# One-hot operations of the experts against a row of numbers in PSUM, four tokens at a time for the first kind, and GELU's result left in PSUM

## Chip, cores, metric

The kernel runs on one core of a Trainium2 chip. A core has TensorE (PE in the profile, its weight loads PEld), VectorE (DVE), ScalarE (ACT), GpSimd (POOL) and a queue for transfers (SP). The metric is device time in microseconds of one execution of the whole kernel.

## What is computed

A transformer of three layers on 256 tokens of width 1024, in float32. Two layers form the first block; the third, the second block, ends in the experts that this case is about. Each token takes 8 heads with 16 of 16384 rows of two tables each, picked by a product of two sets of 128 keys:

```python
def body(hblk):
    q = (hblk @ w_q).reshape(B, TB, PEER_HEADS, 2, PEER_DHALF)
    s = jnp.einsum('btphd,phnd->btphn', q, subkeys).astype(jnp.float32)
    v, i = lax.top_k(s, PEER_TOPK)
    ...
    tv, tj = lax.top_k(cand, PEER_TOPK)
    eidx = jnp.take_along_axis(cidx, tj, axis=-1)
    w = jax.nn.softmax(tv, axis=-1)
    u = w_down[eidx]
    a = jax.nn.gelu(jnp.einsum('btd,btpkd->btpk', hblk, u).astype(jnp.float32))
    vv = w_up[eidx]
    return jnp.einsum('btpk,btpkd->btd', (w * a).astype(hblk.dtype), vv)
```

So a token has 128 pairs (row, column) in a grid of 128 by 128 experts, and a weight for each.

## The kernel before

**Dense experts.** The kernel gathers nothing. It treats the grid as 128 units of 128 experts. For unit `e`, `expert(e)` multiplies the unit's part of `w_down` with h for all 256 tokens: 24 matmuls of 128x256 (three for each of 8 slices of the width, lines 284 to 286, since each operand is split in two float32r parts). `gelu(e, o)` applies GELU to the result o, which lies in one of the PSUM banks 0 to 3 in turn. The result, times the token's weight for each expert, stands in `slots[e]` (128 experts x 256 tokens). After all 128 units, `finish` multiplies the slots with `w_up`.

**Weights of a token.** In the later part of the 128 units, the kernel also builds each token's 128x128 grid of weights: the product of two one-hot matrices. `onehot(t)` makes both on VectorE, each from one `tensor_scalar` over `con`, a tile that holds 0 to 127 in each row: line 1639 compares it with the token's 128 row numbers (one per partition, in `SELT[:, 0, t]`), line 1640 compares it with the column numbers and multiplies by the weights. `weight(t)` is one float32 matmul of the two (line 1648, two records in the trace), into a quarter of one of the banks 4 to 7. When four tokens (a group) fill a bank, `place` distributes it: for the units that have their GELU, VectorE multiplies (line 1657); for the later ones ScalarE copies (line 1659). For a later unit, `gelu` then has two parts: tokens without weights as before (line 1566), tokens with weights through a buffer `gls` in SBUF (line 1569), which VectorE multiplies into the slot (line 1570).

**Order.** Every engine works through its instructions in the order of the program. `expert` calls `token` four times, after each second slice (six matmuls); `token` issues `onehot(t + 3)` and then `weight(t)` when one is due, at a rate that spreads 256 tokens over the units that are left. Here the first weight stands with 81.6 units to go, so 0.79 tokens fall on a call. The stretch from the first weight matmul to the last is called the token stage below.

**Loads.** Each unit's 512 KB come by a transfer into one of four buffers, ScalarE writes the upper part (line 238), and GpSimd the rest (line 240: source minus upper part, both in SBUF). In the stage of `finish` VectorE does that subtraction (line 242).

Of the kernel before, what the change touches and what calls it, by code (L numbers as in the profile page):

```python
# [16 lines left out]
P = 128  # L17
# [13 lines left out]

# ---------------------------------------------------------------- constants of the shapes
def shape_constants():
# [64 lines left out]

# ---------------------------------------------------------------- layout of the inputs
def lay_out(i):  # L100
# [72 lines left out]

# ---------------------------------------------------------------- the stream of weights
RG_YIELD = (1,)
# [3 lines left out]
class Stream:  # L179
    """Weights in the order of their use: loaded ahead, split ahead into two float32r parts."""  # L180

# [18 lines left out]
    def free(self, which, u):  # L200
        """Whether all that reads unit u from its buffer is in the program."""
        return u < 0 or (u < self.done if which == 1 and self.units[u][3] else u < self.busy)

    def buf(self, i, which):
        """The buffer of the ring whose last user is the longest gone, if it is free."""
        r = [x for x in self.rings if x[0] <= i][-1][which]
        j = min(range(len(r)), key=lambda j: self.last.get((which, r[j][0]), -1))
        key = (which, r[j][0])
        if not self.free(which, self.last.get(key, -1)):
            return None  # L210
        self.last[key] = i
        return r[j][1]
# [33 lines left out]
    def take(self, labels):  # L246
        """Units that are used together."""
        self.busy = self.pos
        us = [self.next(*l, hold=True) for l in labels]
        return us  # L250
# [22 lines left out]
class Build:  # L273
    def __init__(self, ctx, tc, I, out, dbg):
        self.ctx, self.tc, self.nc, self.I, self.out, self.dbg = ctx, tc, tc.nc, I, out, dbg

    # ------------------------------------------------------------ helpers
    def dump(self, name, ap):
# [33 lines left out]

    # ------------------------------------------------------------ the whole program
    def run(self):
# [93 lines left out]

    # ------------------------------------------------------------ modulations
    def mods_setup(self, mp):  # L410
# [16 lines left out]
    def first_mods(self):  # L427
        """The first two modulations, on the tensor engine: the rows of silu(c) in two parts, the weights moving."""
        nc, I, W = self.nc, self.I, self.W
# [55 lines left out]
    def dot(self, l, jt, w):  # L485
        """One tile of a modulation: its rows times the row of silu(c)."""
        nc = self.nc
        junk = self.mp.tile([P, D], BF16, name=f"junk{l}_{jt}", tag="junk", bufs=1)
        if l == 2:
            outs = [(2, self.mad2[:, jt:jt + 1])]  # L490
        else:
            outs = [(c, self.mall[:, l, c, jt:jt + 1]) for c in ((0, 1) if l == 0 or jt < 40 else (0,))]
        for c, o in outs:
            nc.vector.scalar_tensor_tensor(junk, w, 1.0, self.cb[c], op0=OP.mult, op1=OP.mult, accum_out=o)  # L494
# [7 lines left out]
    def more(self, pool, end, n=2, stagger=False):  # L502
        """Two more buffers for split weights in a pool that is open until the unit `end`."""
        W = self.W
        self.nmore = getattr(self, "nmore", 0) + 1
        new = [(f"m{self.nmore}_{j}", pool.tile([P, 2, 1024], F32R, name=f"hm{self.nmore}_{j}", bufs=1)) for j in range(n)]
        e = W.index(*end)
        W.ring(W.done, self.raws, self.hls + new)
        if stagger:
            W.ring(e - 4, self.raws, self.hls)  # L510
            W.ring(e - 2, self.raws, new)
        W.ring(e, self.raws, self.hls)
# [59 lines left out]

    # ------------------------------------------------------------ norm and modulation of x into h
    def norm(self, T, l, i):
        """Prepares h = rms(x) * s1 + s0 for the next linear map; l, i name the modulation."""
        self.nT, self.nl, self.ni = T, l, i
        self.ndouble = l == 2 and i == 0
        self.nacc = self.np.tile([P, 512], F32, name="nacc", tag="nacc", bufs=1)
        self.nlast = self.np.tile([P, 512], F32, name="nlast", tag="nlast", bufs=1)
        self.nrow = {}  # L580
        self.nsq, self.nadd = [self.nlast], self.nc.gpsimd
# [38 lines left out]
    def bcast(self, half):  # L620
        """One over the root mean square of each token, in all partitions."""
        R, cols = self.nrow[half]
        rows = [R[:, :P], R[:, P:]] + ([self.bank[7][:, S + j * P:S + (j + 1) * P] for j in range(2)] if self.ndouble else [])
        for o, c in zip(rows, cols):
            self.nc.tensor.matmul(o, c.broadcast_to((P, P)), self.C["ident"], start=True, stop=True)
# [30 lines left out]

    # ------------------------------------------------------------ linear maps
    def group(self, labels, T, early=False):
        """First tiles of a linear map of h, with k outside: it starts with the first rows of h.
        The columns of x run while those of the context are normalised."""  # L660
        W = self.W
# [36 lines left out]
    def tail(self, label, nk, T, gate, last=True, order=None, rest=None):  # L698
        """x += gate * (w^T g): d tiles; the last ones by halves, so that the next norm overlaps them."""
        nc = self.nc  # L700
# [72 lines left out]

    # ------------------------------------------------------------ feed forward
    def ffn(self, l, w, T, nxt, fp, early=False):
# [26 lines left out]

    # ------------------------------------------------------------ first block
    def first_block(self):
# [314 lines left out]

    # ------------------------------------------------------------ second block: retention and sparse attention  # L1120
    def second_mix(self):
        nc, tc, I, W = self.nc, self.tc, self.I, self.W
        T = S
        with tc.tile_pool(name="mix2", bufs=1) as p:
# [55 lines left out]
            def tokens(u, k, c0, n, o):  # L1180
                """Rows of h as the stationary side: n columns from c0 of the unit, for both tiles of tokens."""
                for t in range(2):
# [16 lines left out]
            def blocks(kv):  # L1199
                """The raw keys or values of the blocks, two rows of a block on top of each other."""  # L1200
                Y = p.tile([P, 2, T], F32, name=f"Y{kv}")
# [327 lines left out]

    # ------------------------------------------------------------ second block: the experts  # L1530
    def peer(self, fb):
# [8 lines left out]
        SELT = Xf[:, 0, :768].rearrange("p (a t) -> p a t", a=3)  # L1540
        gls = [Xf[:, 0, 1280:1536], Xf[:, 0, 1536:1792]]
        con = pp.tile([P, P], F32, name="iota")
# [19 lines left out]
        def gelu(e, o):  # L1562
# [4 lines left out]
            if nb:  # L1567
                g = gls[e % 2]
                nc.scalar.activation(g[:, :nb], o[:, :nb], AF.Gelu_apprx_tanh)
            return lambda: nb and nc.vector.tensor_tensor(slots[e][:, :nb], slots[e][:, :nb], g[:, :nb], OP.mult)  # L1570

# [55 lines left out]
        self.ring = [0, 1, 2, 3]  # L1627
        wb = [4, 5, 6, 7]
        SAv = self.SA.rearrange("p (e t) -> p e t", t=S)
        SCv = Xf[:, 0:1, 1792:2048]  # L1630
        SBv = slotB.rearrange("p (e t) -> p e t", t=S)

        ohs = {}

        def onehot(t):
            if t >= T:
                return
            oh = pp.tile([P, 2, P], F32, name="oh", tag="oh", bufs=4)
            nc.vector.tensor_scalar(oh[:, 0], con, SELT[:, 0, t:t + 1], None, op0=OP.is_equal)  # L1639
            nc.vector.tensor_scalar(oh[:, 1], con, SELT[:, 1, t:t + 1], SELT[:, 2, t:t + 1], op0=OP.is_equal, op1=OP.mult)  # L1640
            ohs[t] = oh

        def weight(t):
            if t >= T:
                return
            oh = ohs.pop(t)
            o = self.bank[wb[t // 4 % 4]][:, t % 4 * P:(t % 4 + 1) * P]
            nc.tensor.matmul(o, oh[:, 0], oh[:, 1], start=True, stop=True)  # L1648

        def place(g, e):  # L1650
            """The weights of four tokens go to all experts: those up to e have their activations."""
            bv = self.bank[wb[g % 4]].rearrange("p (t e) -> p e t", e=P)
            ts = slice(4 * g, 4 * g + 4)
# [49 lines left out]
    def topk(self, p, iota, SC, SEL):  # L1703
        """The experts of all tokens and their weights; yields about the vector engine's time in us."""
        nc = self.nc
# [66 lines left out]
    def finish(self, slots, xd, pp):  # L1772
# [17 lines left out]
        def ends():  # L1790
            """What the end needs, in the place of slots that have been used."""
            nc.sync.dma_start(SA[:, :2048], xd)
# [51 lines left out]

# ---------------------------------------------------------------- launch
# [13 lines left out]
```

## Time and profile before

| | before |
|---|---|
| timed runs, median of 3 | 2833.49 us (2833.3 to 2834.64) |
| span of the profiled execution | 2830.7 us |
| TensorE busy | 2731.6 us (97%) |
| VectorE busy | 1903.9 us (67%) |
| GpSimd busy | 505.6 us (18%) |
| bytes read from HBM | 446.35 MB, 158 GB/s over the span |

The span goes from the first to the last instruction. For the profiled execution the profile gives the span and no other time; the median of the timed runs lies 2.8 us above that span. A matmul's record is longer than the distance to the next one, since matmuls are pipelined: "busy" counts the union of the records.

### The profile page before, as it was taken

How to read it: one execution, taken by the hardware profiler on the slowest of the kernel's cores; microseconds unless marked ns; L12 is line 12 of the kernel's file. 1: busy time of each engine (PE TensorE's matmuls, PEld its weight loads, DVE VectorE, ACT ScalarE, POOL GpSimd, SP SyncE). 2: the span in 40 equal slices, each digit the busy share in tenths (PEclk: the TensorE clock that was granted, in tenths of full speed). 3: DMA queues.
4: the chain of work that ended last, by engine and by line, in shares of the span. 5: the costliest groups of instructions: out<-in, count | busy, mean ns of one | idle time of the engine just before them, and what ended most of it. 6: DMA issues, size and time to landing. Idle time of an engine off the chain costs nothing. (4 is left out here: it accounts for less than half of the span.)

```text
span 2830.7 us, 41128 instructions
## 1 busy us (share of the span) xinstructions
PE 2731.6 (97%) x15899; PEld 2352.1 (83%) x15899; DVE 1903.9 (67%) x3580; ACT 1089.4 (38%) x1867; POOL 505.6 (18%) x284
## 2 busy tenths in 40 slices
PE   6999999999999999999999999999999988899998
PEld 4888887678888898888978999779998988888887
DVE  6777764457776565555546556675888999855555
ACT  5322234433222232222344444634443443354554
POOL 1000010020000010000121002331896555400000
PEclk9999999999999999999999999999999999999999
DMA  6555643124555535555344555424554434456664
GB/s 252 183 191 187 194 126 110 54 82 142 184 185 192 175 126 189 191 193 182 110 127 129 191 185 171 161 68 164 181 163 142 133 122 134 129 193 207 193 193 142
DMA packets 129477, 451.41 MB, mean 159 GB/s; under 512 B 16000, under 2 KB 21120, under 8 KB 127744
## 3 DMA queue, kind: packets, MB, share of 16 engines
q1 hardware_dynamic: 129280, 448.77, 49.2%
q8 instruction: 125, 2.05, 0.3%
q14 instruction: 72, 0.59, 0.1%
HBM read 446.35 MB, written 2.10 MB: 158 GB/s over the span
## 5 line engine op out<-in xcount | busy, mean ns | idle before, releaser
L284 PE MATMUL bank<-Hh,hl 128*128 128x256 f32 (+1 forms) x1968 | 663.2, 337 | 6.9 <-ACT Hh L643 5.1
L286 PE MATMUL bank<-Hh,hl 128*128 128x256 f32 (+1 forms) x1968 | 641.9, 326 | 2.7 <-POOL hl L240 2.7
L285 PE MATMUL bank<-Hl,hl 128*128 128x256 f32 (+1 forms) x1968 | 642.6, 327 | 1.7 <-DVE Hl L646 1.6
L238 ACT ACTIVATE hl<-raw 128x1024 fp32r<-128x1024 f32 (+1 forms) x401 | 411.7, 1043 | 280.3 <-DMA raw<-in_w_dram 84.7
L242 DVE TENSOR_TENSOR hl<-raw,hl 128x1024 fp32r<-128x1024 f32 (+1 forms) x316 | 381.4, 1216 | 184.6 <-ACT hl L238 183.9
L284 PEld LDWEIGHTS bank<-Hh,hl 128*128 128x128 f32 x1968 | 375.3, 191 | 51.2 <-issue 11.2
L286 PEld LDWEIGHTS bank<-Hh,hl 128*128 128x128 f32 x1968 | 375.0, 191 | 36.2 <-POOL hl L240 3.3
L285 PEld LDWEIGHTS bank<-Hl,hl 128*128 128x128 f32 x1968 | 375.4, 191 | 34.2 <-DVE Hl L646 2.7
L494 DVE SCALAR_TENSOR_TENSOR junk<-wm,cb 128x1024 bf16<-128x1024 f32 x272 | 332.0, 1221 | 12.2 <-ACT cb L500 7.7
L597 POOL TENSOR_TENSOR nacc<-nlast,nacc 128x256 f32<-128x256 f32 (+1 forms) x56 | 60.9, 1093 | 1342.6 <-issue 848.8
L240 POOL TENSOR_TENSOR hl<-raw,hl 128x1024 fp32r<-128x1024 f32 x85 | 214.6, 2532 | 194.6 <-ACT hl L238 181.9
L284 PE MATMUL bank<-G,hl 128*128 128x512 f32 (+1 forms) x673 | 229.6, 341 | 0.0
L285 PE MATMUL bank<-G,hl 128*128 128x512 f32 (+1 forms) x673 | 228.6, 340 | 0.0
L286 PE MATMUL bank<-G,hl 128*128 128x512 f32 (+1 forms) x673 | 228.5, 340 | 0.0
L310 ACT ACTIVATE G<-silu 128x512 fp32r<-128x512 f32 (+1 forms) x88 | 50.9, 579 | 414.1 <-DVE silu L783 414.1
L783 DVE TENSOR_TENSOR silu<-silu,bank 128x512 f32<-128x512 f32 (+1 forms) x88 | 54.6, 621 | 201.9 <-PE bank L286 197.1
L1807 PE MATMUL bank<-hl,Hh 128*128 128x512 f32 x768 | 179.4, 389 | 0.0
L284 PE MATMUL bank<-Hh,hm 128*128 128x512 f32 (+1 forms) x496 | 177.4, 358 | 0.0
L286 PE MATMUL bank<-Hh,hm 128*128 128x512 f32 (+1 forms) x496 | 177.1, 357 | 0.0
L285 PE MATMUL bank<-Hl,hm 128*128 128x512 f32 (+1 forms) x496 | 176.9, 357 | 0.0
L709 DVE SCALAR_TENSOR_TENSOR X<-bank,mall,X 128x256 f32<-128x256 f32 x192 | 84.5, 479 | 132.8 <-PE bank L286 132.7
L1807 PEld LDWEIGHTS bank<-hl,Hh 128*128 128x128 f32 x768 | 144.2, 188 | 29.9
(350 smaller groups left out, 5327.0 us busy)
## 6 DMA issues: line engine op xcount, KB each, us to landing
raw<-in_w_dram SPq DMA_DIRECT2D x208, 512.0 KB, 4.1
wm<-in_wmod_dram SPq DMA_DIRECT2D x128, 512.0 KB, 4.3
X<-in_wdn_dram SPq DMA_DIRECT2D x64, 512.0 KB, 3.6
raw<-in_wdn_dram SPq DMA_DIRECT2D x64, 512.0 KB, 3.6
X<-in_wup_dram SPq DMA_DIRECT2D x64, 512.0 KB, 3.6
raw<-in_wup_dram SPq DMA_DIRECT2D x64, 512.0 KB, 3.7
raw<-in_w_dram SPq DMA_DIRECT2D x64, 448.0 KB, 3.8
wm<-in_wada_dram SPq DMA_DIRECT2D x48, 512.0 KB, 4.6
```

What stands on the lines that cost most here:

```text
L238: nc.scalar.activation(hl[:, 0, :n], raw[:, :n], AF.Copy)
L240: nc.gpsimd.tensor_tensor(hl[:, 1, :n], raw[:, :n], hl[:, 0, :n].bitcast(F32), OP.subtract)
L242: nc.vector.tensor_tensor(hl[:, 1, :n], raw[:, :n], hl[:, 0, :n].bitcast(F32), OP.subtract)
L284: mm(o, wh, xh, start=start, stop=False)
L285: mm(o, wh, xl, start=False, stop=False)
L286: mm(o, wl, xh, start=False, stop=stop)
L310: nc.scalar.activation(dst[0], src, AF.Copy)
L494: nc.vector.scalar_tensor_tensor(junk, w, 1.0, self.cb[c], op0=OP.mult, op1=OP.mult, accum_out=o)
L597: self.nadd.tensor_tensor(acc, last, acc, OP.add)
L709: nc.vector.scalar_tensor_tensor(x, self.bank_(b, T, half), g[:, d:d + 1], x, op0=OP.mult, op1=OP.add)
L783: nc.vector.tensor_tensor(s, s, self.bank_(bb, T), OP.mult)
L1807: nc.tensor.matmul(acc[t][n], c[:, a, ts], u[:, b, n * 512:(n + 1) * 512], start=e == 0 and a + b == 0, stop=e == P - 1 and a == 1)
```

## The change

`io` is a copy of `con` in bank 4 of PSUM. Both kinds of one-hot matrix are compared with `io`. The first kind is made for four tokens by one `tensor_tensor` of 512 columns, into one of two buffers in X; the second kind stays one `tensor_scalar` per token, now into one of six buffers of its own (four of the double size before). The weights of a group go to three banks in turn, 5 to 7. GELU's result for the tokens with weights overwrites o in its bank, and the multiplication reads it there; `gls` goes.

```diff
-        gls = [Xf[:, 0, 1280:1536], Xf[:, 0, 1536:1792]]
...
-                g = gls[e % 2]
+                g = o
                 nc.scalar.activation(g[:, :nb], o[:, :nb], AF.Gelu_apprx_tanh)
-            return lambda: nb and nc.vector.tensor_tensor(slots[e][:, :nb], slots[e][:, :nb], g[:, :nb], OP.mult)
+            return lambda: nb and nc.vector.tensor_tensor(slots[e][:, :nb], g[:, :nb], slots[e][:, :nb], OP.mult)
...
-        wb = [4, 5, 6, 7]
+        io = self.bank[4][:, :P]
+        nc.vector.tensor_copy(io, con)
+        wb = [5, 6, 7]
...
-            oh = pp.tile([P, 2, P], F32, name="oh", tag="oh", bufs=4)
-            nc.vector.tensor_scalar(oh[:, 0], con, SELT[:, 0, t:t + 1], None, op0=OP.is_equal)
-            nc.vector.tensor_scalar(oh[:, 1], con, SELT[:, 1, t:t + 1], SELT[:, 2, t:t + 1], op0=OP.is_equal, op1=OP.mult)
+            if t % 4 == 0:
+                first = Xf[:, 0, 768 + t // 4 % 2 * 512:][:, :512].rearrange("p (t e) -> p t e", t=4)
+                nc.vector.tensor_tensor(first, io.unsqueeze(1).broadcast_to((P, 4, P)),
+                                        SELT[:, 0, t:t + 4].unsqueeze(2).broadcast_to((P, 4, P)), OP.is_equal)
+                firsts[t // 4] = first
+            oh = pp.tile([P, P], F32, name="oh", tag="oh", bufs=6)
+            nc.vector.tensor_scalar(oh, io, SELT[:, 1, t:t + 1], SELT[:, 2, t:t + 1], op0=OP.is_equal, op1=OP.mult)
...
-            o = self.bank[wb[t // 4 % 4]][:, t % 4 * P:(t % 4 + 1) * P]
-            nc.tensor.matmul(o, oh[:, 0], oh[:, 1], start=True, stop=True)
+            o = self.bank[wb[t // 4 % 3]][:, t % 4 * P:(t % 4 + 1) * P]
+            nc.tensor.matmul(o, firsts[t // 4][:, t % 4], oh, start=True, stop=True)
...
-            bv = self.bank[wb[g % 4]].rearrange("p (t e) -> p e t", e=P)
+            bv = self.bank[wb[g % 3]].rearrange("p (t e) -> p e t", e=P)
```

On VectorE, between the places where units 56 and 57 have their weights, there stood before (line, operation, what it writes and reads, size; in brackets the engines waited for):

```order
L1570 TENSOR_TENSOR slotA_14610<-slotA_14610,X_71 128x28 [waits Activation_49]
L1657 TENSOR_TENSOR slotA_14610<-slotA_14610,bank7_70 128x56x4
L1639 TENSOR_SCALAR oh_17158<-iota_14606,X_71 128x128 [waits PE_49]
L1640 TENSOR_SCALAR oh_17158<-iota_14606,X_71 128x128
L1639 TENSOR_SCALAR oh_17168<-iota_14606,X_71 128x128 [waits PE_49]
L1640 TENSOR_SCALAR oh_17168<-iota_14606,X_71 128x128
L1639 TENSOR_SCALAR oh_17184<-iota_14606,X_71 128x128 [waits PE_49]
L1640 TENSOR_SCALAR oh_17184<-iota_14606,X_71 128x128
L1570 TENSOR_TENSOR slotA_14610<-slotA_14610,X_71 128x32 [waits Activation_49]
L1657 TENSOR_TENSOR slotA_14610<-slotA_14610,bank4_67 128x57x4
```

and now, at the same place (lines 1569, 1642, 1646 and 1663 of the changed kernel are the GELU product, the four tokens' first one-hot matrices, the second kind and the product of `place`):

```order
L1569 TENSOR_TENSOR slotA_14610<-bank2_65,slotA_14610 128x28 [waits Activation_49]
L1663 TENSOR_TENSOR slotA_14610<-slotA_14610,bank6_69 128x56x4
L1642 TENSOR_TENSOR X_71<-bank4_67,X_71 128x512 [waits PE_49]
L1646 TENSOR_SCALAR oh_17130<-bank4_67,X_71 128x128 [waits DVE_49]
L1646 TENSOR_SCALAR oh_17139<-bank4_67,X_71 128x128 [waits DVE_49]
L1646 TENSOR_SCALAR oh_17154<-bank4_67,X_71 128x128 [waits PE_49]
L1569 TENSOR_TENSOR slotA_14610<-bank3_66,slotA_14610 128x32 [waits Activation_49]
L1663 TENSOR_TENSOR slotA_14610<-slotA_14610,bank7_70 128x57x4
L1646 TENSOR_SCALAR oh_17173<-bank4_67,X_71 128x128 [waits PE_49]
```

Three tokens' six operations on `iota` (`con`) have become one on four tokens and four single ones, all of which read bank 4. The GELU product reads a bank where it read X. A one-hot operation waited for the matmul of four tokens back to give its buffer free; now the operation on four tokens waits for the last weight matmul of two groups back, and a single one for that of six tokens back.

On TensorE, where a group's first weight stands, before:

```order
L285 MATMUL bank3_66<-Hl_73,Hh_72 128x256
L286 MATMUL bank3_66<-Hh_72 128x256
L1648 MATMUL bank4_67<-oh_17266 128x128 [waits DVE_49,Activation_49]
L284 MATMUL bank3_66<-Hh_72 128x256
L285 MATMUL bank3_66<-Hl_73,Hh_72 128x256
```

and now:

```order
L285 MATMUL bank3_66<-Hl_73,Hh_72 128x256
L286 MATMUL bank3_66<-Hh_72 128x256
L1654 MATMUL bank5_68<-oh_17232,X_71 128x128 [waits DVE_49,Activation_49]
L284 MATMUL bank3_66<-Hh_72 128x256
L285 MATMUL bank3_66<-Hl_73,Hh_72 128x256
```

Nothing has moved on TensorE. The matmul reads two tiles where it read one, and the ScalarE copy that it waits for is that of the group three back, before four back.

## Rows read from the trace of the kernel before

**Rows 1.** The page's first part, whole span: busy us, share, count.

```profile
PE 2731.6 (97%) x15899; PEld 2352.1 (83%) x15899; DVE 1903.9 (67%) x3580; ACT 1089.4 (38%) x1867; POOL 505.6 (18%) x284
```

**Rows 2.** Chain that ended last, through the token stage: share by line.

```profile
by line: DVE oh L1639 31.5%; DVE oh L1640 30.9%; PE bank L1648 6.6%; PE bank L284 6.5%; PE bank L285 6.3%; PE bank L286 6.3%; DVE slotA L1657 4.2%; DVE slotB L1570 4.2%; DVE slotB L1657 2.0%; issue 1.1%; DVE Hl L242 0.4%; ACT Hl L238 0.3%; 
```

**Rows 3.** Busy time by window: the token stage, a slice of it, and one before.

```profile
core 0: us, PE busy (x) PEld busy (x) DVE busy (x) ACT busy (x) POOL busy (x), PEclk, DMA share, GB/s
2131.43:2465.79 334.36, 300.74 (x2470) 293.09 (x2471) 320.61 (x699) 129.07 (x381) 188.38 (x79) 0.99 0.42 129
2140.00:2160.00 20.00, 19.70 (x168) 19.50 (x168) 18.61 (x40) 8.52 (x27) 12.00 (x6) 1.00 0.41 129
2040.00:2060.00 20.00, 20.00 (x169) 20.00 (x168) 20.00 (x89) 9.31 (x14) 19.24 (x9) 1.00 0.77 218
```

**Rows 4.** That slice for line 1648 alone: PE busy, PEld busy, clock, DMA.

```profile
2140.00:2160.00 20.00, 6.62 (x34) 5.22 (x34) 1.00 0.41 129
```

**Rows 5.** Waits in the token stage: total us, times, longest.

```profile
ACT slotB L1659 <- DVE slotB L1657: 141.4, 45, 6.7
PE bank L1648 <- DVE oh L1640: 33.6, 38, 1.7
```

**Rows 6.** Lines 1639 and 1640: duration ns min/median/max, first and last start.

```profile
L1639 DVE TENSOR_SCALAR oh<-iota,X x256: 268/276/2459, 2128.6 to 2464.7; 128x128 f32<-128x128 f32 x128
L1640 DVE TENSOR_SCALAR oh<-iota,X x256: 329/335/2541, 2128.9 to 2464.9; 128x128 f32<-128x128 f32 x128
```

**Rows 7.** VectorE by line, token stage: count, busy us, mean ns, idle before.

```profile
L1640 DVE TENSOR_SCALAR oh<-iota,X 128x128 f32<-128x128 f32 x255 | 159.0, 623 | 0.0
L1639 DVE TENSOR_SCALAR oh<-iota,X 128x128 f32<-128x128 f32 x255 | 148.0, 580 | 10.6 <-PE bank L1648 10.2
L1657 DVE TENSOR_TENSOR slotA<-slotA,bank 128x272 f32<-128x272 f32 (+16 forms) x63 | 26.1, 414 | 0.0
L1570 DVE TENSOR_TENSOR slotB<-slotB,X 128x80 f32<-128x80 f32 (+45 forms) x58 | 22.4, 386 | 0.0
L1657 DVE TENSOR_TENSOR slotB<-slotB,bank 128x4 f32<-128x4 f32 (+44 forms) x45 | 11.8, 263 | 0.0
```

**Rows 8.** Timeline around 2267: GpSimd, VectorE, TensorE (start, us, engine, line).

```profile
2265.33 2.41 POOL L240 TENSOR_TENSOR Hl<-X,Hl 128x1024 fp32r<-128x1024 f32 x1 [3.40 <-ACT Hl L238]
2267.69 2.36 POOL L240 TENSOR_TENSOR hl<-raw,hl 128x1024 fp32r<-128x1024 f32 x1
...
2265.44 2.38 DVE L1639 TENSOR_SCALAR oh<-iota,X 128x128 f32<-128x128 f32 x1
2267.74 2.40 DVE L1640 TENSOR_SCALAR oh<-iota,X 128x128 f32<-128x128 f32 x1
...
2268.38 0.28 PE L286 MATMUL bank<-Hh 128*128 128x256 f32 x1
2270.20 0.49 PE L1648 MATMUL bank<-oh 128*128 128x128 f32 x2 [1.54 <-DVE oh L1640]
```

**Rows 9.** Timeline around 1899: GpSimd, then VectorE, in an earlier stage.

```profile
1898.69 2.50 POOL L240 TENSOR_TENSOR hl<-raw,hl 128x1024 fp32r<-128x1024 f32 x1
...
1898.89 0.72 DVE L1508 TENSOR_SCALAR ry<-bank,mv,rr 128x128 f32<-128x128 f32 x2
1899.65 1.83 DVE L1510 TENSOR_TENSOR ry<-ry,RG 128x256 f32<-128x256 f32 x1
```

**Rows 10.** Line 1508 (ns min/median/max), and line 783 by shape.

```profile
L1508 DVE TENSOR_SCALAR ry<-bank,mv,rr x8: 401/404/410, 1871.7 to 1906.7; 128x128 f32<-128x128 f32 x8
...
L783 DVE TENSOR_TENSOR silu<-silu,bank 128x512 f32<-128x512 f32 x66 | 45.4, 688 | 169.6 <-PE bank L286 166.5 <-ACT silu L782 3.1
```

**Rows 11.** ScalarE by line, token stage.

```profile
L238 ACT ACTIVATE hl<-raw 128x1024 fp32r<-128x1024 f32 x40 | 43.2, 1080 | 0.0
L1569 ACT ACTIVATE X<-bank 128x4 f32<-128x4 f32 (+39 forms) x79 | 23.4, 296 | 0.0
L1659 ACT ACTIVATE slotB<-bank 128x236 f32<-128x236 f32 (+45 forms) x62 | 18.4, 296 | 145.8 <-DVE slotB L1657 141.4 <-DVE slotA L1657 4.4
```

More of the change, by code (lines that the diff above doesn't have):

```diff
@@ L1631, in peer @@
         SBv = slotB.rearrange("p (e t) -> p e t", t=S)
-        ohs = {}
+        ohs, firsts = {}, {}
         def onehot(t):
```

## The prediction, made before the changed kernel ran

> **What bounds the kernel now.** The page comes first: TensorE is busy 97% of the span, VectorE 67% [rows 1]. Read alone, that says that VectorE's work costs nothing. It is an average over stages, so the next view is the chain of waits through the token stage. There the chain runs 31.5% through line 1639 and 30.9% through line 1640, the two one-hot operations, and only about 6.5% through each line of matmuls [rows 2]. In this stage TensorE follows VectorE.
>
> The windows give the stage its size: 334.36 us, 2470 matmul records, TensorE busy 300.74, VectorE 320.61 (96%), GpSimd 188.38 in 79 operations [rows 3]. TensorE is idle 33.6 us, and the waits give all of it to one cause: the weight matmul waits for a one-hot matrix 38 times [rows 5].
>
> Why is VectorE so busy? A one-hot operation takes 276 ns (line 1639) or 335 (line 1640) at the median, but up to 2459 and 2541 [rows 6], and 580 and 623 in the mean [rows 7]. The timeline shows what the long ones have in common: GpSimd starts its subtraction at 2265.33 and works to 2267.74; a one-hot operation that starts at 2265.44 ends at 2267.82. GpSimd's next runs from 2267.69 to 2270.05, and line 1640's goes from 2267.74 to 2270.14. The weight matmul behind them starts at 2270.20, 1.82 us after the matmul ahead of it [rows 8]. A one-hot operation that meets GpSimd's subtraction stands still until that ends. The bill for the stage: lines 1639 and 1640 take 148.0 + 159.0 = 307.0 us [rows 7], and would take 255 x (0.276 + 0.335) = 155.8 at their medians. The 151 us between are 1.9 us for each of GpSimd's 79 operations: nearly every one holds VectorE for most of its 2.4 us.
>
> **The change, step by step.**
>
> 1. *Does a source in PSUM escape?* Line 1508 is the operation that the second kind becomes: `tensor_scalar`, 128x128, source in a bank, two columns of scalars in SBUF, result in SBUF. Two of them start at 1898.89, inside a GpSimd subtraction (1898.69 to 1901.19), and both are done in 0.72 us; line 1510 behind them, with two sources in SBUF, takes 1.83 us and ends with GpSimd [rows 9]. All eight took 401 to 410 ns [rows 10]. The four-token operation has one source in a bank and one in SBUF, as line 1657 has, whose mean is 414 ns for up to 272 columns, with no long ones in the mean [rows 7]. The GELU product takes that form too. So I take the stall as gone for all three.
>
> 2. *VectorE's own work.* The second kind goes from 335 to 404 ns [rows 6, 10]. The first kind for four tokens is priced by line 783, a product of 512 columns with one source in a bank: 688 ns [rows 10]; bounds are 0.6 (1.5 times line 1657's) and 1.1 us (four times line 1639's median). Four tokens cost 4 x (276 + 335) = 2444 ns before without stalls, and 688 + 4 x 404 = 2304 now. So the merging as such saves 0.14 us a group, 9 us in 64 groups of an engine that is then no longer waited for: nothing. The stage's sum on VectorE becomes 64 x 0.688 + 256 x 0.404 + 26.1 + 11.8 (`place`) + 22.4 (GELU product, as now) = 208 us.
>
> [...]
>
> 3. *TensorE at its own pace.* The slice from 2140 to 2160 has almost no wait: 168 records with 19.70 us busy [rows 3], 34 of them weight matmuls [rows 4]. That is 20.2%, against 512 of 2470 = 20.7% for the stage, so its mix is right. At 168 per 20.00 us the stage takes 2470 / 8.40 = 294.0 us; at 168 per 19.70 it takes 289.6. I take the middle, 292, and a gain of 334.4 - 292 = 42.4. It is more than the 33.6 us of idle, because a matmul's record goes on for some time into each wait.
>
> 4. *What is late next?* The feeding must hold a unit (24 + 6.3 records) every 3.6 us where it held one every 4.1. GpSimd needs 188 of 292 us. ScalarE needs 129 [rows 3]; now it mostly waits for VectorE's product (141.4 us, [rows 5]), and its splits stand behind that, so it is freed too. The slice from 2040 to 2060, before the stage, shows units without weight matmuls: 169 records in 20.00 us with TensorE never idle, at 218 GB/s and with GpSimd busy 19.24 [rows 3]. Feeding at 129 x 334 / 292 = 148 GB/s is well inside that. VectorE at 208 of 292 is the fullest of the three.
>
> 5. *New waits.* A group's first weight now waits for ScalarE's copies of the group three back, not four. Those copies stand, at the latest, behind the GELU of unit e-1 when the earlier group ended in unit e; the weight stands at least six matmuls into e for that group's last token, and five tokens later, at 0.79 tokens for six matmuls: at least 36 more. So there are 42 matmuls, 42 x 20 / 168 = 5.0 us, and the weights between them, 6 x 2 x 20 / 168 = 1.4. In that time ScalarE must do the GELU's two parts (0.26 for the part in the slot, taken as 0.3; 0.296), a split (1.08), and up to three copies (0.3 each), and VectorE the GELU product (0.39) and `place` (0.41 + 0.26) [rows 7, 11]: 3.6 us together. It fits with 2.8 us over. The bank of a GELU result is free only after VectorE's product; its next user is four units later. The buffers of the one-hot matrices got longer, six and eight tokens against four. GELU's write to a bank instead of SBUF has no row; even 0.1 us either way, 79 times, is 8 us of ScalarE's idle 205.
>
> 6. *Start.* One copy into bank 4 and the first operation on four tokens stand ahead of the first weight: at most 0.41 (a `place` product of twice its columns) + 0.69 + 0.40, less the 0.61 of before, 0.9 us once. I count 0.5.
>
> Sum: -42.4 + 0.5, about -42. In the profile's terms 2830.7 becomes 2788.7; the timed median lies 2.8 us above the span, so 2833.5 - 42 = **2791.5 us**.
>
> **Rivals.**
>
> *TensorE stays half starved* (chance 0.11). One in-order VectorE serves TensorE, ScalarE and the slots; a product that waits for a GELU holds back the one-hot matrices queued behind it. VectorE stands only three tokens ahead in the program, 3 x 292 / 256 = 3.4 us. For it: VectorE now waits 10.2 us in all before line 1639 for the matmul that frees a buffer [rows 7], so it is ahead at times and late at others. Against it: without stalls it is 71% busy. If half the gain is lost: 2833.5 - 21 = 2812.
>
> *The change doesn't do what it says* (0.04). Scalars and one input still come from SBUF. If GpSimd holds such operations too, the bill of 1.9 us for each subtraction stays, VectorE's own work is the same within 9 us, and the time is 2833 within 5. Against it stand the two operations in rows 9, few as they are.
>
> *Slower: three banks* (0.03). If ScalarE's copies came later than the 6.4 us of step 5, TensorE would wait at each group's first weight, 61 times. ScalarE's longest wait for VectorE is 6.7 us now [rows 5], but that one is made by the stalls that go. To be slower by over 0.2% it must eat the gain and 5.7 us more, 48 us, so 0.8 us at every group, copies at 7.2 us or later. At 1 us a group the time would be 2833.5 - 42 + 61 = 2852.
>
> **How the numbers follow.** The forecast, that TensorE runs the stage at its own pace, has the rest, 0.82. Its own range comes from step 3: at 289.6 us and no start cost 2788.7; at 294.0 us and 0.9 us, 2794. If only the idle time of 33.6 us comes back, 2800. Since a tenth of the chance lies near 2812 and some of the forecast's may lie just above its own range, I give 2785 to 2802. A change of 0.2%, 5.7 us, is about what a measurement of this kernel can tell from none. Faster by more than that: 0.82 + 0.11 = 0.93; within it 0.04; slower 0.03.
>
> **What the profile after should show.** The two kinds of one-hot operation with a mean within 5% of their median, about 404 and 690 ns, and no 2.4 us among them, though GpSimd's subtractions still take 2.4. VectorE busy near 208 us in the token stage, which lasts 290 to 296 us. The waits of the weight matmul for a one-hot matrix below 5 us. ScalarE's wait for VectorE's product smaller, its wait for the end of a unit on TensorE larger. The chain of waits through the stage on the matmul lines. The prediction is wrong if one-hot operations still reach 2.4 us (step 1), if VectorE's chain is still there without stalls (step 2), or if weight matmuls wait for ScalarE (step 5); outside the token stage nothing should move by more than a microsecond or two.

## The result, and the profile after

The changed kernel takes 2789.68 us (median of 4 runs, 2787.89 to 2790.71) against 2833.39 before (median of 4, 2829.94 to 2834.64): a ratio of 0.984, 95% interval 0.983 to 0.986. The forecast was 2791.5.

The page's first part of the changed kernel (busy us, share of the span, count):

```profile
span 2786.0 us, 40945 instructions
...
PE 2721.2 (98%) x15899; PEld 2348.9 (84%) x15899; DVE 1760.2 (63%) x3389; ACT 1103.4 (40%) x1867; POOL 506.5 (18%) x284
```

TensorE's busy time has fallen by 10 us and its share risen by a point; VectorE has lost 144 us. The page alone would not say which of these bought 44.7 us of span. The chain of waits through the token stage does:

```profile
by line: PE bank L284 26.3%; PE bank L285 26.2%; PE bank L286 26.1%; PE bank L1654 19.4%; DVE oh L1646 0.4%; DVE Hl L242 0.4%; ACT Hl L238 0.4%; DVE slotA L1663 0.2%; DVE slotB L1569 0.2%; issue 0.1%; DVE slotB L1663 0.1%; ACT slotB L1665 0
```

In [rows 2] the two one-hot lines had 62% of the stage's chain; now line 1646 has 0.4%, and the four lines of TensorE have 98%. The window of the token stage (from the first weight matmul to the last; busy us and count by engine, granted clock, DMA share, GB/s):

```profile
core 0: us, PE busy (x) PEld busy (x) DVE busy (x) ACT busy (x) POOL busy (x), PEclk, DMA share, GB/s
2128.25:2421.16 292.91, 291.52 (x2470) 291.32 (x2471) 177.81 (x507) 142.56 (x381) 190.22 (x80) 1.00 0.48 148
```

Against [rows 3]: the same 2470 matmul records in 292.91 us where they took 334.36. TensorE is idle 1.4 us of it, where it was idle 33.6. VectorE is busy 178 us where it was busy 321. GpSimd's time has not changed.

The two kinds of one-hot operation, by line (duration in ns: minimum, median, maximum):

```profile
L1646 DVE TENSOR_SCALAR oh<-bank,X x256: 394/402/414, 2127.7 to 2420.2; 128x128 f32<-128x128 f32 x128
```

```profile
L1642 DVE TENSOR_TENSOR X<-bank,X x64: 681/691/692, 2127.1 to 2414.7; 128x512 f32<-128x512 f32 x64
```

This answers to [rows 6]: the maximum is 414 ns where it was 2541, though GpSimd's 80 subtractions fill 65% of the stage. The waits in the stage (total us, times, longest):

```profile
DVE X L1642 <- PE bank L1654: 90.4, 61, 2.2
ACT slotB L1565 <- PE bank L286: 70.7, 50, 2.2
ACT slotB L1665 <- DVE slotB L1663: 33.4, 26, 3.8
DVE oh L1646 <- PE bank L1654: 16.1, 36, 1.0
PEld bank L1654 <- DVE oh L1646: 1.6, 1, 1.6
```

Who waits for whom has turned round. VectorE now waits for TensorE, 90 us before the four-token operation and 16 before the single one, for its buffers. TensorE's weight matmul waits once for VectorE, 1.4 us (its weight load, the last row, 1.6); in [rows 5] it waited 33.6. The slots lie in two tiles, slotA and slotB: for those in slotB, ScalarE's wait for VectorE's product in `place` went from 141 to 33 us, and its line 1565 waits 71 us for the end of a unit on TensorE.

### The profile page after: what moved, and what is told of

It reads as the page before. It is cut to its first block, busy times and chain, and to the rows that moved or that the text cites. A ratio compares the mean times of both kernels' runs of the same rounds, so it can differ in the third digit from the quotient of the medians.

```text
span 2786.0 us, 40945 instructions
## 1 busy us (share of the span) xinstructions
PE 2721.2 (98%) x15899; PEld 2348.9 (84%) x15899; DVE 1760.2 (63%) x3389; ACT 1103.4 (40%) x1867; POOL 506.5 (18%) x284
```

## Experiments

The prediction's account: operations of VectorE with all their tensors in SBUF stand still while GpSimd subtracts; with one source in PSUM they don't; the four-token operation, the longer buffers, the three banks and the GELU part have next to no share. The rivals: the merging or the buffers did it; VectorE's queue remains a bound; three banks cost something. Times are medians; the kernel before beside the first four runs took 2833.4 (13 runs), beside the last four 2838.4 (9 runs, 2828.6 to 2843.6).

**The row of numbers back in SBUF.** Edit of the changed kernel:

```diff
-        io = self.bank[4][:, :P]
-        nc.vector.tensor_copy(io, con)
+        io = con
```

> The changed kernel, with the row of numbers read from its tile in SBUF again; one operation for four tokens, the longer buffers, three banks and GELU's result in PSUM stay. If operations with all sources in SBUF are held by GpSimd's subtraction (the prediction's account), the long one-hot operations of 2.4 us come back, VectorE is above 95% busy in the token stage, that stage takes 325 to 340 us and the kernel 2818 to 2838. If the gain came from fewer operations or longer buffers, it stays at 2790 within 4.

Measured: 2826.5 us, ratio to before 0.997 (0.995 to 0.998). The window of its token stage, with the columns of the window above, the two one-hot lines by busy us and mean ns, and the wait of the weight matmul:

```profile
2134.54:2460.40 325.86, 303.84 (x2470) 299.99 (x2471) 307.23 (x507) 138.48 (x381) 195.64 (x79) 0.97 0.42 132
```

```profile
L1645 DVE TENSOR_SCALAR oh<-iota,X 128x128 f32<-128x128 f32 x255 | 197.6, 815 | 1.1 <-PE bank L1653 1.1
L1641 DVE TENSOR_TENSOR X<-iota,X 128x512 f32<-128x512 f32 x63 | 74.7, 1186 | 9.9 <-PE bank L1653 9.8
```

```profile
PE bank L1653 <- DVE oh L1645: 17.5, 12, 3.3
```

The stage is back at 326 us with VectorE 94% busy (above 95% was expected). The means are 815 and 1186 ns; 255 x 0.334 + 63 x 0.680 = 128 us at their own medians (334 and 680), so of 272 us, 144 are standing still: 1.8 us for each of GpSimd's 79 operations, against 1.9 before. Fewer operations did not lower that bill. What the merging, the longer buffers, the three banks and GELU's result in PSUM give together without the PSUM source is 7 us; which of them, this run doesn't tell.

The 7 us are not the worth of the shorter waiting alone. TensorE is idle 22.0 us of the stage where it was idle 33.6, but the granted clock of the stage is 0.97 where it was 0.99 before. The waits for a one-hot matrix have become fewer and longer: 12 of up to 3.3 us, where [rows 5] has 38 of up to 1.7. What a granted clock below 1 is for the matmuls, the profile of the kernel before shows once: after the 1.97 us that TensorE waited ahead of its first weight, matmuls of 256 columns stand 0.21 us apart from 2132.2 to 2135.4, where they are else 0.12 apart, and the profile gives 0.50 for the clock of that stretch, 0.83 for the 10 us from 2130. That is 1.7 us of missing clock; every later 10 us of that stage has 1.00. By its 0.97 the run here misses 0.03 x 325.86 = 10 us, an estimate from a rounded figure (8 to 11). After which of its waits the clock falls was not shown.

**The row of numbers in PSUM, and nothing else.** Edit of the kernel before:

```diff
-        wb = [4, 5, 6, 7]
+        io = self.bank[4][:, :P]
+        nc.vector.tensor_copy(io, con)
+        wb = [5, 6, 7]
...
-            nc.vector.tensor_scalar(oh[:, 0], con, SELT[:, 0, t:t + 1], None, op0=OP.is_equal)
+            nc.vector.tensor_scalar(oh[:, 0], io, SELT[:, 0, t:t + 1], None, op0=OP.is_equal)
...
-            nc.vector.tensor_scalar(oh[:, 1], con, SELT[:, 1, t:t + 1], SELT[:, 2, t:t + 1], op0=OP.is_equal, op1=OP.mult)
+            nc.vector.tensor_scalar(oh[:, 1], io, SELT[:, 1, t:t + 1], SELT[:, 2, t:t + 1], op0=OP.is_equal, op1=OP.mult)
```

(and the remainder by 3 in place of 4 in `weight` and `place`, since bank 4 is taken).

> The kernel before, with the row of numbers in bank 4 and three banks for the weights, and nothing else: two operations per token, four buffers, GELU's result through SBUF. If the held operations are the cause, this alone gives nearly all of the gain: 2788 to 2797, one-hot operations at about 345 and 404 ns with no long ones, while some of the 80 GELU products, still with two sources in SBUF, now take up to 2.5 us. If the merging is what counts, the time stays within 6 us of 2833.

Measured: 2792.4 us, ratio 0.985 (0.982 to 0.988). Window of its token stage, and lines of VectorE:

```profile
2132.58:2425.83 293.25, 290.46 (x2469) 289.71 (x2470) 264.20 (x700) 129.56 (x381) 193.16 (x80) 1.00 0.48 148
```

```profile
L1642 DVE TENSOR_SCALAR oh<-bank,X 128x128 f32<-128x128 f32 x255 | 101.5, 398 | 0.0
L1641 DVE TENSOR_SCALAR oh<-bank,X 128x128 f32<-128x128 f32 x255 | 87.1, 341 | 25.9 <-PE bank L1650 25.2
L1570 DVE TENSOR_TENSOR slotB<-slotB,X 128x80 f32<-128x80 f32 (+45 forms) x58 | 59.2, 1021 | 0.0
L1570 DVE TENSOR_TENSOR slotA<-slotA,X 128x8 f32<-128x8 f32 (+15 forms) x21 | 24.2, 1153 | 0.0
```

This one step gives 41 of the 44 us. Line 1642 (the second kind) and line 1641 (the first) have means of 398 and 341 ns. GpSimd's hold has moved to what is left with two sources in SBUF: the GELU products have means of 1021 and 1153 ns, 83.4 us in all where they took 26.2 (22.4 in [rows 7] and 3.8 in slotA). VectorE is 90% busy, and TensorE still hardly waits (it is idle 2.8 us of the stage).

**GELU's result through SBUF again.** Edit of the changed kernel (with two tiles `gls` of 256 columns, and `bufs=4` for the second kind):

```diff
-                g = o
+                g = gls[e % 2]
...
-            return lambda: nb and nc.vector.tensor_tensor(slots[e][:, :nb], g[:, :nb], slots[e][:, :nb], OP.mult)
+            return lambda: nb and nc.vector.tensor_tensor(slots[e][:, :nb], slots[e][:, :nb], g[:, :nb], OP.mult)
```

> The changed kernel, with GELU's result through two buffers in SBUF as before (and four buffers of the second one-hot kind instead of six, for the room). By the prediction's account the products are held by GpSimd now, up to 2.5 us each, perhaps 40 of 80, some 50 us of VectorE's time; but VectorE has 115 us to spare in the token stage, so the time stays at 2788 to 2795. If the products' place on VectorE's in-order queue matters, the weight matmul waits again and the time is above 2800.

Measured: 2791.4 us, ratio 0.985 (0.982 to 0.988). Window of its token stage:

```profile
2129.06:2424.00 294.94, 291.76 (x2470) 291.39 (x2471) 243.07 (x507) 129.63 (x381) 190.56 (x80) 1.00 0.48 147
```

VectorE's busy time rises by 65 us, the stage by 2, the kernel by 1 to 2 us, which the runs hardly tell from nothing. So the GELU part of the change is work off the path.

**GpSimd's subtraction on a quarter of the columns.** Edit of the kernel before:

```diff
-                    nc.gpsimd.tensor_tensor(hl[:, 1, :n], raw[:, :n], hl[:, 0, :n].bitcast(F32), OP.subtract)
+                    m = n // 4 if label[0] == "wdn" else n
+                    nc.gpsimd.tensor_tensor(hl[:, 1, :m], raw[:, :m], hl[:, 0, :m].bitcast(F32), OP.subtract)
```

> The kernel before, in which GpSimd subtracts only 256 of the 1024 columns of each unit of the down weights; the other columns keep what the buffer held, so the experts' products are not the reference's. VectorE's instructions are those of before. If GpSimd's subtraction is what holds the one-hot operations, they are held 0.6 us at most, VectorE falls to about 220 to 240 us in the token stage, and the kernel takes 2788 to 2800. If the long operations have another cause, it stays at 2833 within 6.

Measured: 2781.1 us, ratio 0.981 (0.979 to 0.984). Window of its token stage, and the one-hot lines:

```profile
2124.10:2414.97 290.87, 289.37 (x2470) 289.17 (x2471) 194.14 (x699) 130.74 (x381) 59.98 (x79) 1.00 0.47 148
```

```profile
L1641 DVE TENSOR_SCALAR oh<-iota,X 128x128 f32<-128x128 f32 x255 | 91.5, 359 | 0.0
L1640 DVE TENSOR_SCALAR oh<-iota,X 128x128 f32<-128x128 f32 x255 | 80.5, 316 | 93.5 <-PE bank L1649 92.7
```

VectorE's program is that of the kernel before, with everything in SBUF; only GpSimd holds it for less long. The stage falls to 290.9 us, and the one-hot means to 316 and 359 ns. So it is GpSimd's operation that holds VectorE, and a shorter one holds it less: over the medians of the kernel before, the one-hot lines now stand 16 us (80.5 + 91.5 - 155.8), 0.2 us for each subtraction of 0.76 us, where it was 1.9 us for one of 2.4. The bill fell by more than the length did; VectorE is idle for 93 us of this stage and so less often in the way, which is an argument and was not measured. The expected time was missed by 7 us on the low side and VectorE's 220 us by 26: the shorter subtractions also help ahead of the token stage (the first weight stands at 2124.1 us, in the two profiles of the changed kernel at 2128.2 and 2131.0). There no matmul of the units waits for GpSimd's subtraction in this run; in the kernel before those of line 286 wait 5.2 us for it, and TensorE is busy 24.79 of the 30.00 us between 2080 and 2110. The last run below takes up that stretch.

**Four banks for the weights.** The changed kernel, run again as the measure for the next three runs:

> The changed kernel itself, as the measure for the three runs beside it: 2789 within 3.

Measured: 2790.5 us (5 runs, 2787.8 to 2791.4). The edit:

```diff
-        self.ring = [0, 1, 2, 3]
+        self.ring = [0, 1, 2]
...
-        wb = [5, 6, 7]
+        wb = [3, 5, 6, 7]
```

(and the remainder by 4 in place of 3 in `weight` and `place`; the units' products have three banks for it.)

> The changed kernel with four banks for the weights and three instead of four for the units' products. If three banks cost nothing (the prediction's step 5), the time is that of the changed kernel within 3 us. If weight matmuls lose time on ScalarE's copies, it is lower by more than 3.

Measured: 2790.5 us. Window of its token stage:

```profile
2130.51:2423.45 292.94, 291.54 (x2470) 291.35 (x2471) 177.97 (x507) 142.57 (x381) 190.19 (x80) 1.00 0.48 148
```

Nothing moves, neither the stage nor the waits in it: three banks were enough.

**The second kind twice.** The changed kernel, in which line 1646 stands twice in a row:

> The changed kernel, in which each one-hot operation of the second kind is done twice, into the same buffer: 256 operations more of 0.40 us, about 0.32 apart. VectorE goes from 178 to about 260 us busy of the stage's 293. If VectorE is off the path (the prediction), the time stays within 4 us of the changed kernel; if TensorE follows VectorE's queue even without stalls, it rises by 20 us or more.

Measured: 2791.9 us, 1.4 more than the changed kernel. Window of its token stage, and the wait of the weight matmul:

```profile
2129.16:2424.78 295.62, 291.76 (x2470) 291.39 (x2471) 272.92 (x762) 141.62 (x381) 190.10 (x80) 1.00 0.48 147
```

```profile
PE bank L1655 <- DVE oh L1647: 3.9, 2, 3.1
```

VectorE has 95 us more to do, is busy 273 us of 295.6 (about 260 were expected), and the stage is 2.7 us longer; a single wait of 3.1 us ahead of the last weights is about that much. With no stalls in it (means of 403 and 410 ns for the two lines), a VectorE that is 92% busy still feeds TensorE; before, one that was 96% busy with stalls of 2.4 us in it cost 33.6 us of idle.

**The same step just ahead of the token stage.** In the changed kernel's profile TensorE was idle 5.2 us between 2080 and 2110, where VectorE chooses the experts. The window (busy us by engine, clock, DMA), GpSimd's timeline and VectorE's, of the changed kernel:

```profile
2080.00:2110.00 30.00, 24.79 (x198) 23.77 (x198) 29.83 (x13) 14.10 (x21) 30.00 (x9) 1.00 0.43 130
```

```profile
2076.92 4.57 POOL L240 TENSOR_TENSOR Hh<-X,Hh 128x1024 fp32r<-128x1024 f32 x1
2081.44 4.43 POOL L240 TENSOR_TENSOR Hl<-X,Hl 128x1024 fp32r<-128x1024 f32 x1
```

```profile
2076.94 2.28 DVE L1760 TENSOR_TENSOR cand<-abf,iota 128x2048 f32<-128x2048 f32 x1
2079.25 4.38 DVE L1763 TENSOR_TENSOR cand<-cand,i16f 128x2048 f32<-128x2048 f32 x1
```

Here each holds the other. The comparison of line 1760, two sources in SBUF, is through in 2.28 us, and GpSimd's subtraction beside it takes 4.57, to 2081.49. The product of line 1763 stands until then and takes 4.38, to 2083.63, and GpSimd's next one stands until that and takes 4.43. The edit, in `topk` of the changed kernel, puts the indices and the 16 numbers in banks 6 and 7, which are free by then:

```diff
-        v16, i16, i16f = two("v16", [P, 16, 16]), two("i16", [P, 16, 16], U32), two("i16f", [P, 16, 16])
+        v16, i16 = two("v16", [P, 16, 16]), two("i16", [P, 16, 16], U32)
+        i16f = [self.bank[6][:, t * S:(t + 1) * S].rearrange("p (a n) -> p a n", a=16) for t in range(2)]
+        nc.vector.tensor_copy(self.bank[7][:, :16], iota[:, :16])
...
-        io = iota[:, :16].unsqueeze(1).broadcast_to((P, P, 16))
+        io = self.bank[7][:, :16].unsqueeze(1).broadcast_to((P, P, 16))
```

> The changed kernel, with the same step taken in the choice of the experts, just ahead of the token stage: the 16 numbers and the indices that its four comparisons and four products of 2048 columns read go to two banks. In the changed kernel's profile GpSimd's subtractions take up to 4.5 us there and TensorE is idle 5.2 us between 2080 and 2110. If those are held by VectorE's two sources in SBUF, GpSimd's stay at 2.4, the comparisons and products fall from 3.9 and 4.4 to 2.3 us, and the kernel gains 4 to 6 us: 2784 within 3. If GpSimd is late there for another reason, it stays at 2789.

Measured: 2783.9 us (5 runs, 2780.0 to 2785.3), 6.6 below the changed kernel's 2790.5 beside it, with no overlap of the runs. The window of 2080 to 2110, GpSimd's timeline and the two lines of VectorE:

```profile
2080.00:2110.00 30.00, 30.00 (x253) 30.00 (x252) 21.72 (x14) 17.01 (x26) 25.20 (x11) 1.00 0.62 187
```

```profile
2076.19 2.41 POOL L240 TENSOR_TENSOR Hh<-X,Hh 128x1024 fp32r<-128x1024 f32 x1 [0.47 <-ACT Hh L238]
2079.06 2.41 POOL L240 TENSOR_TENSOR Hl<-X,Hl 128x1024 fp32r<-128x1024 f32 x1 [0.47 <-ACT Hl L238]
```

```profile
L1765 DVE TENSOR_TENSOR cand<-cand,bank 128x2048 f32<-128x2048 f32 x4 | 9.1, 2287 | 0.1
L1762 DVE TENSOR_TENSOR cand<-abf,bank 128x2048 f32<-128x2048 f32 x4 | 9.1, 2278 | 0.0
```

TensorE is busy all 30.00 us where it was 24.79, GpSimd's subtractions are at 2.41, and the products and comparisons take 2.28 us, the product above 4.38. This version beats both kernels.

## Why the prediction was right

*Step 1* (a source in PSUM escapes) held without exception: 320 one-hot operations, none above 0.70 us, and no GELU product above 0.42. It rested on two operations in [rows 9], and the runs bear it out from both sides: the PSUM source alone gives the gain (2792.4 us), taking it away returns the loss (2826.5), and with the sources left in SBUF a shorter operation of GpSimd gives the gain too (2781.1). Two columns of scalars in SBUF beside a source in a bank don't bring the hold back: line 1646 has them, and its maximum is 414 ns. Line 1639, with a single tensor in SBUF and one column of scalars, was held (up to 2459 ns [rows 6]) like the GELU products with two tensors in SBUF (up to 2558 ns in the run with the row alone in PSUM); which of its operands makes it so, no run here separates.

*Step 2*, the prices: 404 was forecast for the second kind and 402 measured, 688 for the first and 691 measured. Against the median with the row in SBUF, 335 ns [rows 6], the second kind takes 402 - 335 = 67 ns more. VectorE's total was mis-sized: 208 us forecast, 178 measured. The lines of VectorE in the stage (count, busy us, mean ns, idle before):

```profile
L1646 DVE TENSOR_SCALAR oh<-bank,X 128x128 f32<-128x128 f32 x255 | 95.1, 403 | 17.1 <-PE bank L1654 16.1
L1642 DVE TENSOR_TENSOR X<-bank,X 128x512 f32<-128x512 f32 x63 | 43.5, 691 | 90.4 <-PE bank L1654 90.4
L1663 DVE TENSOR_TENSOR slotA<-slotA,bank 128x272 f32<-128x272 f32 (+16 forms) x63 | 26.1, 415 | 0.0
L1569 DVE TENSOR_TENSOR slotB<-bank,slotB 128x80 f32<-128x80 f32 (+45 forms) x58 | 18.2, 314 | 1.1 <-ACT bank L1568 1.1
L1663 DVE TENSOR_TENSOR slotB<-slotB,bank 128x4 f32<-128x4 f32 (+44 forms) x45 | 12.0, 266 | 0.0
L1569 DVE TENSOR_TENSOR slotA<-bank,slotA 128x8 f32<-128x8 f32 (+15 forms) x21 | 3.9, 186 | 1.4 <-ACT bank L1568 1.4
```

They add up to 199 us, near the 208 of the working; but records of VectorE that follow each other overlap (four of line 1646, of 0.40 us each, take 1.36 us from 2127.75 on), and the window counts their union. This could be seen beforehand: the rows of [rows 7] add up to 367 us, where the window in [rows 3] has 320.61. It changed nothing, since the run with the second kind twice shows that 273 us are still enough.

*Step 3*, TensorE's own pace: 292 forecast, 292.9 measured. The slice of the kernel before without waits was a good measure for the whole stage. Of the stage's gain, 32.2 us are idle time of TensorE and 9.2 us busy time. The forecast put all of the second part down to records that go on into a wait. About 1.7 us of it is the granted clock, by the estimate above: 0.99 over the stage before, 1.00 now. The other 7.5 us are 0.2 us for each of the 38 waits, near the 0.16 by which a record of 0.28 us outlasts the distance of 0.12 to the next.

*Steps 4 and 5*: ScalarE, GpSimd and the transfers kept up, and no weight matmul waited for ScalarE's copies; a fourth bank changes nothing. GELU's write to a bank was allowed 8 us of ScalarE's time and took 13 (last section), off the path.

*Step 6*: the 0.5 us for the start had the wrong sign, because the kernel before was held there too. Its first operation of line 1640 stood under a subtraction of GpSimd for 2.38 us, and TensorE waited 1.97 us for the first weight; now it waits 0.59. From VectorE's last copies ahead of the one-hot operations to the first weight it took 3.81 us before and takes 2.43 in both profiles of the changed kernel: 1.4 us gained. The first weight stands 3.2 us earlier than before in one of them and 0.5 in the other. The rest of this lies ahead of those copies, which start 1.8 us earlier in the one and 0.9 us later in the other, with the same program up to there: a difference between executions, of the size of the microsecond or two that the prediction allowed outside the stage.

*The sum*: the stage gives 41.5 us, 42.4 were forecast. The spans of the two profiles differ by 44.7 us: 41.5 from the stage, 1.4 from its start, 1.8 from what lies ahead of it. The profiled execution of the changed kernel is the fastest of its four, 1.8 us below their median, and the medians differ by 43.7. The mechanism was right; that the sum came within 2 us is in part luck, as the start had the wrong sign and executions of one kernel differ by more than that (2829.9 to 2834.6 before). Of the rivals, the half-starved TensorE, the slip of the three banks and the change without effect are each ruled out by a run.

## What to carry to other kernels

A busy engine can be a waiting one: compare an operation's mean with its median (580 and 276 ns for line 1639) before believing its share. Where the long ones start and end with another engine's operation, look at where both have their tensors; one constant operand moved to PSUM, at 67 ns an operation, took away some 150 us of VectorE's standing still, and the operand that is used most often is the one to move. The same hold makes the other engine the loser when it comes second (GpSimd's subtraction took 4.57 us beside line 1760, and 2.41 once that line's source was in a bank), so each place where VectorE and GpSimd both work with all tensors in SBUF deserves a look.

## What the runs showed that was not expected

With GELU's result in a bank the records of ScalarE got shorter, and yet the engine is busy for longer. ScalarE by line in the token stage of the changed kernel:

```profile
L238 ACT ACTIVATE hl<-raw 128x1024 fp32r<-128x1024 f32 x40 | 42.1, 1051 | 0.0
L1568 ACT ACTIVATE bank<-bank 128x4 f32<-128x4 f32 (+39 forms) x79 | 20.5, 259 | 2.5
```

Against [rows 11]: 259 ns for the same 79 GELUs where they took 296, and 1051 for a split where it took 1080. But ScalarE's busy time in the stage is 142.6 us where it was 129.1 [rows 3], and it is 129.6 in the run that differs from the changed kernel by GELU's result through SBUF and four buffers of the second kind for six. The records run into each other less: around 2305 us in the kernel before, a unit's second GELU starts 0.16 us after its first and the split 0.15 us after that; around 2302 us in the changed kernel it is 0.29 and 0.19. Over 79 units the 0.17 us more are 13 us. Why the next operation starts later is open. ScalarE was not on the path, so this cost nothing, but a shorter record is not a cheaper operation.

The hold is also not shared out when there are fewer operations to hit: with 320 one-hot operations instead of 512, all sources in SBUF, each of GpSimd's still cost VectorE 1.8 us.
